# Two edits in a hybrid backbone kernel: GLA's zero-padded queries copied by ScalarE from one product for both directions, and rotary embedding over two token tiles an instruction

## The chip, the core and the metric

The kernel runs on one core of one Trainium2 chip. The time is in device microseconds, from one execution of the whole program; a stated time is the median of several runs. The engines are TensorE (PE, with its weight loads shown apart as PEld), VectorE (DVE), ScalarE (ACT), GpSimd (POOL) and SyncE (SP, which issues the transfers). Each engine works through its own instructions strictly in the order in which the program holds them.

## The reference

Two layers of a diffusion backbone, over 1024 latent tokens and 256 context tokens of width 1024. Each layer norms and modulates its input, projects it with one matrix of 2,592 columns, and feeds three groups of heads: a convolution module (width 31), windowed attention with rotary embedding (8 query heads of 64, 2 key heads), and gated linear attention (GLA) in both directions. Their outputs go through gates and one output projection. The parts that the change touches are these:

```
def _apply_rope(x, cos, sin):
    half = ATTN_HEAD_DIM // 2                       # 32
    rot = concatenate([-x[..., half:], x[..., :half]], axis=-1)
    return x * cos + rot * sin

def _gla_chunked(q, k, v, log_a, s0):               # chunks of 64 tokens, 4 heads, dk = 32, dv = 64
    b = cumsum(log_a within the chunk)
    q_in = q * exp(b)
    k_in = k * exp(-b)
    att = where(causal, q_in @ k_in.T, 0)           # per head
    o = att @ v + q_in @ s                          # s: the state that enters the chunk
```

The backward direction does the same on flipped tokens, and the two outputs are added, normed and gated. All of it is in 32-bit floats.

## The kernel before, in words

Tokens come in ten tiles of 128: tiles 0 and 1 are the context, 2 to 9 the latent stream. A projection works on groups of 256 columns (`GROUPS`), whose products are three matmul passes over high and low halves of the operands. Some groups leave their output with columns on the partitions and tokens along the free axis (`t_group`), others with tokens on the partitions, two tiles at a time (`tok_group`). `mix` is a large buffer with columns on the partitions; in it row group 2 holds GLA's queries, 3 its keys, 4 and 5 the running sums b of the forward and the backward direction, 6 and 7 the states and later GLA's output.

The order of all instructions is made by a planner while the program is built. The work is split into lanes (Python generators). `Model` keeps a clock for each engine, with a price for each instruction by its shape, and the time at which each piece of a buffer is written and last touched; `loop` takes, at each step, the ready lane of the lowest priority number, lets it issue up to its next `yield`, and moves on. A lane that yields with no condition goes on when the model thinks that what it issued is done. The prices are fixed formulas: `150 + 2.1 n` ns for a POOL product of n elements a partition, `75 + n / 0.96` for a DVE product, `n / 1.2 + 93` for an ACT instruction that reads SBUF. They know nothing of one engine holding up another at a memory port. If a price changes, the order of all that comes after may change on each engine. The hardware then runs the instructions in that order, with semaphores between engines where one needs another's data.

What lies beside the change in `phase_a`, in both layers: while PE runs the groups 10 (v and the low-rank gate), 8 (GLA's q and k), 5 (attention's k and v), 3 and 4 (attention's q), DVE works through the 62 instructions of the convolution (`conv_taps`, each issued when the model has DVE idle), and lanes of GLA run on all engines.

Rotary embedding: `ev_qk_b` takes a pair of tiles from PSUM to an SM buffer with one ACT copy, turns each latent tile with `rope` on POOL (four instructions a tile: the swapped halves times the sines into a borrowed WR buffer, the tile times the cosines in place, a subtract on the first halves and an add on the second), and sends the pair to DRAM through SP. For group 5 the turned part is 2 heads a tile (K, 128 elements a partition), for groups 3 and 4 it is 4 heads (Q, 256 elements). Context tiles are not turned. There are 4 latent pairs in each of three groups in each of two layers, 24 in all.

GLA: `gla_states` makes the chunk states (it has a POOL product of keys and decay, 128x512, that PE then transposes). `gla_out` makes the output of one token tile; two lanes of it run beside each other, over 10 tiles in layer 0 and 8 in layer 1. For each tile it makes exp(b/16) and exp(-b/16) for both directions in `w` (`ws`, an SM buffer), multiplies the keys into the second two, and multiplies the queries into `qx`, a buffer for each direction in which head h has its 32 partitions filled and the rest stays zero, so that one matmul serves four heads. Then PE makes the scores, DVE masks and adds them, PE makes the output, and further steps norm it.

Nearly every line of the profile says L43: all instructions go through one wrapper, `issue` at line 43. Instructions are told apart by engine, tile names and shapes. Rope is POOL `WR<-SM,SM` (sines), `SM<-SM,SM` (cosines) and `SM<-SM,WR` (subtract, add), with 128x128, 128x128 and 128x64 for K and 128x256, 128x256 and 128x128 for Q. The states' product is POOL `SM<-SM,mix 128x512`; GLA's key products are POOL `SM<-SM,mix 128x128`, its query products DVE `SM<-SM,mix 32x128`, its exponentials ACT `SM<-mix 128x128`. The conv taps are DVE `mix<-U,small,mix 128x1295` in layer 0 and `128x1024` in layer 1.

Of the kernel before, what the change touches and what calls it, by code (L numbers as in the profile page):

```python
# [12 lines left out]
ACTF = mybir.ActivationFunctionType  # L13
ALU = mybir.AluOpType
# [12 lines left out]
def col(t):  # L27
    return t if t < 256 else t + GAP
# [136 lines left out]
class Hybrid:  # L165
# [717 lines left out]
                self.flag(f"v{l}.{i}")  # L883
        return ev

    def rope(self, x, nh, blk, tmp):

        nc = self.nc
        x4 = x.rearrange("p (h a b) -> p h a b", a=2, b=32)
        t4 = tmp.rearrange("p (h a b) -> p h a b", a=2, b=32)  # L890
        cos, sin = [self.rt[:, s * 256 + blk * 32:s * 256 + blk * 32 + 32][:, None, None, :].to_broadcast([128, nh, 2, 32]) for s in range(2)]
        e = nc.gpsimd
        e.tensor_tensor(t4, x4[:, :, ::-1, :], sin, op=ALU.mult)
        e.tensor_tensor(x4, x4, cos, op=ALU.mult)
        e.tensor_tensor(x4[:, :, 0], x4[:, :, 0], t4[:, :, 0], op=ALU.subtract)
        e.tensor_tensor(x4[:, :, 1], x4[:, :, 1], t4[:, :, 1], op=ALU.add)

    def ev_qk_b(self, l, name, dst, nh):

        def ev(i0, p):  # L900
            nc = self.nc
            yield self.need("SM"), self.need("WR", 1, 1), f"rope{l}"
            s, tmp = self.sm(512), self.get("WR")
            s3 = s.rearrange("p (s c) -> p s c", s=2)
            nc.scalar.activation(s3, p, ACTF.Copy)
            yield
            if i0 >= 2:
                for r in range(2):
                    self.rope(s3[:, r, 0:nh * 64], nh, i0 + r - 2, tmp[:, r * 256:r * 256 + nh * 64])
            self.free(tmp)  # L910
            yield
            nc.sync.dma_start(dst[i0:i0 + 2].rearrange("s p c -> p s c"), s3)
            self.free(s)
            for i in (i0, i0 + 1):
                self.flag(f"{name}{l}.{i}")
        return ev
# [204 lines left out]
    def gla_out(self, l, i, qx, v):  # L1121
        nc = self.nc
        o = col(i * 128)
        yield self.need("SM", 2), self.rest(v), f"T{l}.0.{self.hslot(i)[0]}"
        self.load_vz(i, v)
        ws, A = self.sm(512), self.sm(512)
        w = ws.rearrange("p (a t) -> p a t", a=4)
        for d in range(2):
            b = self.mix(4 + d, slice(o, o + 128))
            nc.scalar.activation(w[:, d], b, ACTF.Exp, scale=1.0 / 16.0)  # L1130
            nc.scalar.activation(w[:, 2 + d], b, ACTF.Exp, scale=-1.0 / 16.0)
        yield self.at(ws)
        for d in range(2):
            nc.gpsimd.tensor_tensor(w[:, 2 + d], w[:, 2 + d], self.mix(3, slice(o, o + 128)), op=ALU.mult)
            for h in range(4):
                r = slice(32 * h, 32 * h + 32)
                nc.vector.tensor_tensor(qx[d][r, h], w[r, d], self.mix(2, slice(o, o + 128), r), op=ALU.mult)
        yield None, self.bank_need("tr")
        at = self.bank_get("tr")
        for d in range(2):  # L1140
            for c in range(2):
                nc.tensor.matmul(at[64 * c:64 * c + 64, d * 256:(d + 1) * 256], w[:, 2 + d, 64 * c:64 * c + 64],
                                 qx[d][:, :, 64 * c:64 * c + 64], start=True, stop=True, tile_position=(0, 64 * c))
        yield
        for d in range(2):
            nc.vector.copy_predicated(self.zz[:, d].rearrange("p (h t) -> p h t", h=4),
                                      self.gmask[:, d:d + 1].to_broadcast([128, 4, 64]),
                                      at[:, d * 256:(d + 1) * 256].rearrange("p (h t) -> p h t", h=4))
        self.free(at)
        nc.vector.tensor_tensor(A[:, 0:256], self.zz[:, 0], self.zz[:, 1], op=ALU.add)  # L1150
        yield None, self.bank_need("ac"), self.at(v)
        ob = self.bank_get("ac")
        om = ob[:, 0:256]
        for c in range(2):
            rs = slice(64 * c, 64 * c + 64)
            ch = 2 * i + c
            for h in range(4):
                oo = om[rs, h * 64:(h + 1) * 64]
                kw = dict(tile_position=(0, 64 * c))
                nc.tensor.matmul(oo, qx[0][:, h, rs], self.S(0, ch), start=True, stop=False, **kw)  # L1160
                nc.tensor.matmul(oo, qx[1][:, h, rs], self.S(1, ch), start=False, stop=False, **kw)
                nc.tensor.matmul(oo, A[:, h * 64:(h + 1) * 64], v[:, h, c], start=False, stop=True, **kw)
        yield
        om3 = om.rearrange("p (h v) -> p h v", h=4)
        sq = A[:, 256:512]
        nc.scalar.activation(sq, om, ACTF.Square)
        yield
        ss = self.ti(4)
        nc.vector.tensor_reduce(ss, sq.rearrange("p (h v) -> p h v", h=4), axis=mybir.AxisListType.X, op=ALU.add)
        r = self.rstd(ss, 1.0 / 64.0, 4)  # L1170
        yield
        nc.vector.tensor_tensor(sq.rearrange("p (h v) -> p h v", h=4), om3, r[:, :, None].to_broadcast([128, 4, 64]), op=ALU.mult)
        self.free(ob)
        yield None, self.bank_need("tr")
        tp = self.bank_get("tr")
        for j in range(2):
            nc.tensor.transpose(tp[:, j * 128:(j + 1) * 128], sq[:, j * 128:(j + 1) * 128], self.idf)
        yield
        for j in range(2):
            nc.scalar.activation(self.mix(6 + j, slice(o, o + 128)), tp[:, j * 128:(j + 1) * 128], ACTF.Copy,  # L1180
                                 scale=self.gw[:, l, j:j + 1])
        self.free(tp, ws, A)
        self.flag(f"gla{l}.{i}")
# [573 lines left out]
def _tables():  # L1757
    f = np.float32
    n_freq = 16
    inv = (f(10000.0) ** (-np.arange(n_freq, dtype=f) / f(n_freq))).astype(f)  # L1760
    r = np.repeat(np.arange(16, dtype=f), 64)
    c = np.tile(np.arange(64, dtype=f), 16)
    ang = np.concatenate([r[:, None] * inv, c[:, None] * inv], axis=-1).astype(f)
    rope = np.stack([np.cos(ang), np.sin(ang)]).astype(f)
    rope = rope.reshape(2, 8, 128, 32).transpose(2, 0, 1, 3)
    q = np.arange(128)[:, None]
    k = np.arange(128)[None, :]
    z = np.zeros((128, 128), f)
    prev = np.where(k >= q, 0.0, NEG).astype(f)
    nxt = np.where(k <= q, 0.0, NEG).astype(f)  # L1770
    amask = np.concatenate([z, z, prev, z, nxt], axis=1)
    s = (np.arange(128) % 64)[:, None]
    t = np.arange(64)[None, :]
    gm = np.stack([s <= t, s >= t], axis=1).astype(f).reshape(128, 128)
    sel = np.zeros((128, 2), f)
    for j in range(0, 128, 32):
        sel[j:j + 2] = [[1, 0], [0, 1]]
    return dict(rope=rope, amask=amask, gmask=gm, sel=sel)
# [56 lines left out]
```

## Time and profile before

| | |
|---|---|
| median of 3 runs | 1350.08 us (1346.76 to 1352.33) |
| profiled execution, its time | 1350.69 us |
| its span, from the first to the last instruction | 1348.9 us |
| mean clock granted to TensorE | 0.977 |
| rope and GLA beside the projections, layer 0 | about 185 to 345 us of the span |
| the same, layer 1 | about 894 to 1040 us |

A row of the groups of instructions has: line, engine, operation, output and inputs by tile name, their shapes, the count, then the busy time and the mean ns of one, then the idle time ahead of them and what ended it. A row of a timeline has: start, length, engine, line, operation, tiles and shapes, count, and in brackets the idle time ahead of the first and what ended it. Instructions of one kind in a row are merged, so a length over several of them includes the gaps. A row of waits has: who waited, for whom, total us, how often, the longest. Each number comes from one profiled execution.

### The profile page before, as it was taken

What the parts mean: (1) busy time and instruction counts of PE and PEld (TensorE: products, weight loads), DVE (VectorE), ACT (ScalarE), POOL (GpSimd) and SP (SyncE); (2) the same over time, 40 slices, a digit from 0 to 9 for tenths busy, and PEclk for the clock granted to TensorE, in tenths of its full rate; (3) what the DMA queues carried; (4) which work ended last, traced back from release to release, by engine and by line L of the source; (5) the groups of instructions that cost most, each with busy time, mean ns of one, the idle gap of its engine ahead of it and who ended that gap; (6) DMA issues with size and microseconds to landing.
All of it is one profiled execution on the core that took longest, in us unless ns stands there. A gap on an engine that the chain in (4) does not pass through costs nothing. (4 is left out here: it accounts for less than half of the span.)

```text
span 1348.9 us, 24464 instructions
## 1 busy us (share of the span) xinstructions
PE 1253.7 (93%) x9198; PEld 1089.8 (81%) x9198; DVE 962.9 (71%) x1856; ACT 560.2 (42%) x1251; POOL 542.9 (40%) x769
## 2 busy tenths in 40 slices
PE   5999997889999999899999889988899999999997
PEld 3678886778788777779988879977787888898997
DVE  5835894888556577777776676896966478887864
ACT  3711431112223456456652461341112256676751
POOL 1410065956223334434341132056792335645430
PEclk9999988999999999899999989989999999999999
DMA  9453113222114333432113441113232113311112
GB/s 328 143 151 102 47 32 99 59 73 74 29 32 126 120 102 106 137 106 67 48 40 110 139 168 56 53 40 104 69 81 54 39 43 102 98 44 52 63 36 79
DMA packets 113239, 116.48 MB, mean 86 GB/s; under 512 B 38464, under 2 KB 81760, under 8 KB 113120
## 3 DMA queue, kind: packets, MB, share of 16 engines
q1 hardware_dynamic: 113120, 114.92, 28.2%
q8 instruction: 72, 1.18, 0.4%
q14 instruction: 47, 0.39, 0.1%
HBM read 95.47 MB, written 19.42 MB: 85 GB/s over the span
## 5 line engine op out<-in xcount | busy, mean ns | idle before, releaser
L43 PE MATMUL ps<-H,WS 128*128 128x512 f32 x1344 | 339.1, 399 | 3.6 <-ACT U L43 1.7
L43 PEld LDWEIGHTS ps<-H,WS 128*128 128x128 f32 x1344 | 245.1, 189 | 64.2 <-issue 10.0
L43 PE MATMUL ps<-WS,H 128*128 128x256 f32 x1704 | 258.3, 294 | 8.1 <-DVE H L43 4.7
L43 ACT ACTIVATE SM<-ps 128x512 f32<-128x512 f32 (+3 forms) x180 | 92.6, 517 | 397.8 <-PE ps L43 284.2
L43 PEld LDWEIGHTS ps<-WS,H 128*128 128x128 f32 x1704 | 232.1, 198 | 21.4 <-issue 10.2
L43 PE MATMUL ps<-idr,SM 128*128 128x128 f32 (+1 forms) x1076 | 150.5, 273 | 38.1 <-POOL SM L43 25.5
L43 DVE SCALAR_TENSOR_TENSOR mix<-U,small,mix 128x1295 f32<-128x1295 f32 (+1 forms) x120 | 177.6, 1526 | 0.2
L43 PEld LDWEIGHTS ps<-idr,SM 128*128 128x128 f32 (+1 forms) x1076 | 124.1, 143 | 62.2 <-POOL SM L43 29.6
L43 DVE SCALAR_TENSOR_TENSOR H<-ps,H 128x512 fp32r<-128x512 f32 x160 | 105.7, 681 | 46.3 <-ACT H L43 46.1
L43 ACT ACTIVATE SM<-SM,stat 128x641 f32<-128x641 f32 (+2 forms) x144 | 110.5, 769 | 56.4 <-DVE stat L43 43.0
L43 ACT ACTIVATE H<-ps 128x512 fp32r<-128x512 f32 x176 | 99.4, 597 | 80.5 <-PE ps L43 73.9
L43 POOL TENSOR_TENSOR SM<-SM,SM 128x256 f32<-128x256 f32 (+4 forms) x91 | 72.8, 808 | 149.0 <-ACT SM L43 112.5
L43 POOL TENSOR_TENSOR tir<-tir,mhalf 128x1 f32<-128x1 f32 (+2 forms) x55 | 44.9, 820 | 197.8 <-DVE tir L43 173.4
L43 DVE CUSTOM_DVE_ANT_0 SM<-ps,SM,small 128x640 f32<-128x640 f32 (+2 forms) x128 | 102.3, 809 | 25.5 <-PE ps L43 24.7
L43 POOL TENSOR_TENSOR SM<-SM,WR 128x128 f32<-128x128 f32 (+2 forms) x117 | 90.8, 793 | 21.4 <-DVE SM L43 14.2
L43 PE MATMUL ps<-H,H 128*128 128x256 f32 x552 | 97.5, 286 | 0.0
L43 PE MATMUL ps<-H 128*128 128x512 f32 x320 | 97.0, 409 | 0.2 <-DVE H L43 0.2
L43 PE MATMUL ps<-SM,SM 128*32 128x128 f32 (+4 forms) x764 | 81.3, 295 | 12.5 <-DVE SM L43 7.8
L43 PEld LDWEIGHTS ps<-H,H 128*128 128x128 f32 x552 | 81.6, 189 | 1.4 <-issue 0.4
L43 POOL TENSOR_SCALAR SM<-SM,tir 128x640 f32<-128x640 f32 (+2 forms) x77 | 67.7, 892 | 28.5 <-DVE tir L43 18.0
L43 PE MATMUL ps<-WS,SM 128*128 128x256 f32 x248 | 70.2, 283 | 0.0
L43 PE MATMUL ps<-H,SM 128*128 128x256 f32 x248 | 69.4, 280 | 0.0
(150 smaller groups left out, 2121.9 us busy)
## 6 DMA issues: line engine op xcount, KB each, us to landing
WR<-in_w_in_dram SPq DMA_DIRECT2D x80, 256.0 KB, 3.9
WR<-in_w_mod_dram SPq DMA_DIRECT2D x64, 256.0 KB, 3.1
WR<-in_w_out_dram SPq DMA_DIRECT2D x32, 256.0 KB, 3.4
SM<-vd SPq DMA_DIRECT2D x116, 64.0 KB, 2.4
x<-SM SPq DMA_DIRECT2D x20, 256.0 KB, 2.3
SM<-x SPq DMA_DIRECT2D x20, 256.0 KB, 4.3
qd<-SM SPq DMA_DIRECT2D x18, 256.0 KB, 2.2
mix<-in_x_dram SPq DMA_DIRECT2D x8, 512.0 KB, 8.3
```

The lines of the kernel that those rows point to most:

```text
L43: r = getattr(self._e, op)(*a, **k)
```

## The change

In `rope`, a call now takes both tiles of a pair: the tables' columns of two neighbouring blocks are read as one pattern with a tile axis. There are two products with the sines (one for each half, in place of one with the halves swapped by a negative step), one with the cosines over both tiles, one subtract and one add: five POOL instructions for a pair in place of eight. In `gla_out`, the exponentials take both directions in one ACT instruction; one DVE product multiplies the queries into both directions and another the keys, 128 partitions by 256 elements each; then ACT copies the eight 32-partition pieces into `qx`. POOL has no product in `gla_out` any more.

```diff
-    def rope(self, x, nh, blk, tmp):
-        nc = self.nc
-        x4 = x.rearrange("p (h a b) -> p h a b", a=2, b=32)
-        t4 = tmp.rearrange("p (h a b) -> p h a b", a=2, b=32)
-        cos, sin = [self.rt[:, s * 256 + blk * 32:s * 256 + blk * 32 + 32][:, None, None, :].to_broadcast([128, nh, 2, 32]) for s in range(2)]
-        e = nc.gpsimd
-        e.tensor_tensor(t4, x4[:, :, ::-1, :], sin, op=ALU.mult)
-        e.tensor_tensor(x4, x4, cos, op=ALU.mult)
-        e.tensor_tensor(x4[:, :, 0], x4[:, :, 0], t4[:, :, 0], op=ALU.subtract)
-        e.tensor_tensor(x4[:, :, 1], x4[:, :, 1], t4[:, :, 1], op=ALU.add)
+    def rope(self, x, t, nh, blk):
+        e = self.nc.gpsimd
+        cos, sin = [self.rt[:, s * 256 + blk * 32:s * 256 + blk * 32 + 64].rearrange("p (r b) -> p r b", b=32)[:, :, None, :] for s in range(2)]
+        x5, t5 = [z.rearrange("p s (h a b) -> p s h a b", a=2, b=32) for z in (x, t)]
+        for a in range(2):
+            e.tensor_tensor(t5[:, :, :, a], x5[:, :, :, 1 - a], sin.to_broadcast([128, 2, nh, 32]), op=ALU.mult)
+        x4 = x.rearrange("p s (g b) -> p s g b", b=32)
+        e.tensor_tensor(x4, x4, cos.to_broadcast([128, 2, 2 * nh, 32]), op=ALU.mult)
+        for a, op in ((0, ALU.subtract), (1, ALU.add)):
+            e.tensor_tensor(x5[:, :, :, a], x5[:, :, :, a], t5[:, :, :, a], op=op)
...
-                for r in range(2):
-                    self.rope(s3[:, r, 0:nh * 64], nh, i0 + r - 2, tmp[:, r * 256:r * 256 + nh * 64])
+                self.rope(s3[:, :, 0:nh * 64], tmp.rearrange("p (s c) -> p s c", s=2)[:, :, 0:nh * 64], nh, i0 - 2)
...
-        for d in range(2):
-            b = self.mix(4 + d, slice(o, o + 128))
-            nc.scalar.activation(w[:, d], b, ACTF.Exp, scale=1.0 / 16.0)
-            nc.scalar.activation(w[:, 2 + d], b, ACTF.Exp, scale=-1.0 / 16.0)
-        yield self.at(ws)
-        for d in range(2):
-            nc.gpsimd.tensor_tensor(w[:, 2 + d], w[:, 2 + d], self.mix(3, slice(o, o + 128)), op=ALU.mult)
+        both = self.mix(slice(4, 6), slice(o, o + 128))
+        for a in range(2):
+            nc.scalar.activation(w[:, 2 * a:2 * a + 2], both, ACTF.Exp, scale=(1.0 - 2 * a) / 16.0)
+        yield self.at(ws)
+        for a in range(2):
+            nc.vector.tensor_tensor(w[:, 2 * a:2 * a + 2], w[:, 2 * a:2 * a + 2],
+                                    self.mix(2 + a, slice(o, o + 128))[:, None, :].to_broadcast([128, 2, 128]), op=ALU.mult)
+        yield
+        for d in range(2):
             for h in range(4):
                 r = slice(32 * h, 32 * h + 32)
-                nc.vector.tensor_tensor(qx[d][r, h], w[r, d], self.mix(2, slice(o, o + 128), r), op=ALU.mult)
+                nc.scalar.activation(qx[d][r, h], w[r, d], ACTF.Copy)
```

## The prediction

> **What bounds the kernel now.** The page's first lines come first, and then the list of who waited for whom, for TensorE (PE) alone.
>
> ```profile
> span 1348.9 us, 24464 instructions
> PE 1253.7 (93%) x9198; PEld 1089.8 (81%) x9198; DVE 962.9 (71%) x1856; ACT 560.2 (42%) x1251; POOL 542.9 (40%) x769
> PE ps L43 <- POOL SM L43: 26.4, 14, 8.7
> PE ps L43 <- DVE SM L43: 15.2, 16, 2.0
> ```
>
> PE is busy for 93% of the span, so an edit that takes no matmul away can win at most the 95.2 us in which PE stands (1348.9 - 1253.7), and what a lowered clock costs. The edit touches products on POOL and DVE, and those are the two longest entries of PE's waits: 26.4 and 15.2 us. The timeline of PE shows where they lie; the number in brackets is the idle time ahead of the instruction.
>
> ```profile
> 212.52 1.12 PE L43 MATMUL ps<-idr,SM 128*128 128x128 f32 x4 [8.68 <-POOL SM L43]
> 250.87 0.66 PE L43 MATMUL ps<-idr,SM 128*128 128x128 f32 x4 [4.09 <-POOL SM L43]
> 298.82 0.65 PE L43 MATMUL ps<-SM,SM 128*64 128x256 f32 x4 [1.87 <-DVE SM L43]
> 301.35 1.12 PE L43 MATMUL ps<-SM,SM 128*64 128x256 f32 x4 [1.87 <-DVE SM L43]
> 918.30 0.66 PE L43 MATMUL ps<-idr,SM 128*128 128x128 f32 x4 [2.96 <-POOL SM L43]
> 967.44 1.82 PE L43 MATMUL ps<-SM,SM 128*64 128x256 f32 x12 [0.92 <-POOL SM L43]
> 969.95 0.65 PE L43 MATMUL ps<-SM,SM 128*64 128x256 f32 x4 [0.70 <-DVE SM L43]
> 988.64 0.41 PE L43 MATMUL ps<-idr,SM 128*128 128x128 f32 x2 [1.05 <-DVE SM L43]
> ```
>
> The first four lie in layer 0 and the last four in layer 1, both times in the stretch where rope, the conv taps and GLA run beside the projections. What POOL and DVE did ahead of the first wait:
>
> ```profile
> 197.49 1.27 POOL L43 TENSOR_TENSOR WR<-SM,SM 128x128 f32<-128x128 f32 x1 [4.49 <-ACT SM L43]
> 198.84 1.60 POOL L43 TENSOR_TENSOR SM<-SM,SM 128x128 f32<-128x128 f32 x1
> 200.52 3.02 POOL L43 TENSOR_TENSOR SM<-SM,WR 128x64 f32<-128x64 f32 x2
> 206.97 3.01 POOL L43 TENSOR_TENSOR SM<-SM,WR 128x64 f32<-128x64 f32 x2
> 209.94 3.75 POOL L43 TENSOR_TENSOR SM<-SM,mix 128x512 f32<-128x512 f32 x2
> 213.66 0.45 POOL L43 TENSOR_TENSOR WR<-SM,SM 128x128 f32<-128x128 f32 x1
> 195.40 15.94 DVE L43 SCALAR_TENSOR_TENSOR mix<-U,small,mix 128x1295 f32<-128x1295 f32 x10
> ```
>
> PE waits for gla_states' product at 209.94, and that stands on POOL behind a K pair of rope: eight instructions from 197.49 to 209.98, 1.56 us each. The same 128x128 instruction takes 0.45 us at 213.66, after the taps. While DVE issues ten taps in 15.94 us (1.59 each), POOL gets one instruction through per tap, whatever its size between 64 and 128 elements. So in this stretch the **number** of POOL instructions sets the time, more than their elements do.
>
> **Part one, rope.** A pair of tiles goes from eight instructions to five: two sine products and a subtract and an add over both tiles, and one cosine product twice as long. Elements stay the same. Without taps beside it, a Q pair's instruction and one of 512 elements are these:
>
> ```profile
> 260.51 0.73 POOL L43 TENSOR_TENSOR WR<-SM,SM 128x256 f32<-128x256 f32 x1
> 231.32 1.29 POOL L43 TENSOR_TENSOR WS<-WR,WS 128x512 fp32r<-128x512 f32 x1 [2.59 <-ACT WS L43]
> ```
>
> 256 to 512 elements costs 0.56 us more, so 2.2 ns an element and 0.17 us fixed. Three instructions fewer are 0.5 us a pair there, 24 pairs in both layers, 12 us of POOL, and hidden: PE does not wait for POOL in such places. Beside taps, three instructions fewer are worth three tap slots. K pair at 197.49: five slots, four of 1.6 and one, now 256 elements, of about 1.9 (below), are 8.3 us in place of 12.5: **4.2 us** off the 8.68. The next late thing is the product itself, 3.75 us for the two directions, so about 4.5 us of the wait stay.
>
> The second wait:
>
> ```profile
> 237.51 0.92 POOL L43 TENSOR_TENSOR WR<-SM,SM 128x256 f32<-128x256 f32 x1
> 241.00 2.00 POOL L43 TENSOR_TENSOR WR<-SM,SM 128x256 f32<-128x256 f32 x1
> 243.08 1.89 POOL L43 TENSOR_TENSOR SM<-SM,SM 128x256 f32<-128x256 f32 x1
> 248.29 2.52 POOL L43 TENSOR_TENSOR SM<-SM,mix 128x512 f32<-128x512 f32 x1
> 240.64 11.54 DVE L43 SCALAR_TENSOR_TENSOR mix<-U,small,mix 128x1295 f32<-128x1295 f32 x6
> 208.00:212.00 4.00, 0.00 (x0) 0.00 (x0) 3.34 (x3) 0.00 (x0) 4.00 (x3) 0.50 0.22 72
> 275.00:300.00 25.00, 21.46 (x224) 19.39 (x220) 21.54 (x37) 5.82 (x18) 14.92 (x20) 0.99 0.20 55
> 375.00:400.00 25.00, 25.00 (x154) 20.86 (x153) 15.70 (x37) 5.74 (x13) 8.01 (x8) 1.00 0.15 44
> 252.00:256.00 4.00, 3.97 (x31) 3.29 (x32) 3.15 (x9) 0.16 (x1) 3.77 (x6) 0.63 0.22 50
> ```
>
> The Q pair fills POOL from 237.51 to 248.29. Two sine products of about 1.0 us, a cosine of 512 elements of some 2.0 (1.29 alone, 2.52 beside a tap at 248.29), and two of 1.95 (the mean of 2.00 and 1.89) make 7.9 us in place of 10.8: **2.8 us** off the 4.09. The last four rows are stretches of the span: length, busy time of PE, its weight loads, DVE, ACT and POOL, then the clock granted to PE, DMA share and GB/s. The clock stood at half in the long wait and at a mean of 0.63 after the second, which cost 0.37 x 4 = 1.5 us of PE. A wait of 1.3 us would not bring this (a wait of 1.87 us lies in the stretch at 0.99), so **1.5 us** more. After the first wait the clock stays lowered, as 4.5 us still exceeds 4.09.
>
> In layer 1 the wait of 2.96 us ends on the same product behind a K pair.
>
> ```profile
> 915.04 1.32 POOL L43 TENSOR_TENSOR SM<-SM,SM 128x128 f32<-128x128 f32 x1
> 916.99 1.26 POOL L43 TENSOR_TENSOR SM<-SM,mix 128x512 f32<-128x512 f32 x1
> ```
>
> Three slots of 1.32 us are 4.0 us, more than the wait: **3.0 us**. Rope's product goes out by the same SP transfer as before, only earlier, and the WR buffer that it borrows is back earlier for the weights.
>
> The Trainium skill ("SBUF — State Buffer", "Who interferes with whom") says that a DVE instruction with two SBUF inputs and a GpSimd instruction that reads SBUF hold each other out for the whole of the instruction. By that a tap and a 128-element product would take turns, and the slot would be 1.59 + 0.45 = 2.04 us, so the K pair would give 1.9 us more than by the row's 1.6; here the row decides, since 1.6 us is what the slots took.
>
> **Part two, GLA.** Of each of the 18 token tiles it takes eight 32x128 products from DVE and two 128x128 from POOL, and puts two 128x256 products on DVE and eight 32x128 copies on ACT; four exponentials of 128 become two of 256.
>
> ```profile
> L43 DVE TENSOR_TENSOR SM<-SM,mix 32x128 f32<-32x128 f32 x144 | 61.9, 430 | 4.6 <-ACT SM L43 2.4
> L43 POOL TENSOR_TENSOR SM<-SM,mix 128x128 f32<-128x128 f32 x36 | 18.0, 522 | 11.8 <-issue 6.3 <-ACT SM L43 5.0 <-POOL SM L43 0.6
> L43 DVE TENSOR_TENSOR SM<-SM 128x256 f32<-128x256 f32 x18 | 8.7, 486 | 0.8
> L43 ACT ACTIVATE SM<-SM 128x256 f32<-128x256 f32 x14 | 5.4, 415 | 5.0 <-DVE SM L43 4.9
> 265.31 1.70 ACT L43 ACTIVATE SM<-mix 128x128 f32<-128x128 f32 x8
> 290.01 4.52 DVE L43 TENSOR_TENSOR SM<-SM,mix 32x128 f32<-32x128 f32 x8
> 296.05 5.15 DVE L43 TENSOR_TENSOR SM<-SM,mix 32x128 f32<-32x128 f32 x8
> 294.57 1.57 DVE L43 SCALAR_TENSOR_TENSOR mix<-U,small,mix 128x1295 f32<-128x1295 f32 x1
> ```
>
> DVE: 144 x 0.430 = 61.9 us go, 36 x 0.486 = 17.5 us come, so 44 us less. POOL loses 18.0 us. ACT: eight 128-element exponentials in a row take 1.70 us, 0.21 each; a copy of 32x128 has as many elements a partition, so eight copies are 1.7 us a tile. The exponentials fall from 0.85 to at most 2 x 0.415 = 0.83. ACT gets 18 x 1.7 = 31 us more, on an engine that is busy 42%. What hides them is that ACT stands idle most of this time (it is busy 5.82 us in the 25 from 275); without that cover it is the 31 us.
>
> On the path lie the two waits of 1.87 us. The eight products of a tile last 4.52 us from 290.01, a tap follows, and those of the next tile last 5.15 us from 296.05; PE waits for both halves of them. After: two products of 0.49 to 1.0 us for either tile, with the 1.57 us tap still between them or behind, put the second tile's at about 294.5 at the latest (290.0 + 2.0 + 1.6 + 1.0), and its copies 1.7 us later at 296.2, ahead of the 296.95 at which PE began to wait (298.82 - 1.87). Both waits would go, 3.7 us; I take **3.0 us**, as the extra hand-over to ACT and back, and what stands ahead on ACT, is not in any row here. In layer 1 the 0.92 us wait for POOL's product goes with it, and the 0.70 us for DVE's: **1.6 us**. The 1.05 us at 988.64 I leave in.
>
> The copies wait on DVE at the head of ACT's queue. Queued behind them are the PSUM evacuations of the Q groups, GLA's squares and the scaled copies to mix; for the evacuations PE's next bank waits.
>
> **The sum** is 4.2 + 2.8 + 1.5 + 3.0 + 3.0 + 1.6 = 16.1 us. Every edit also changes the planner's costs, so it lays out all instructions behind the first K pair anew: its prices for a tile are 683 in place of 1,667 ns on DVE, nothing in place of 838 on POOL, and some 2,210 in place of 800 on ACT. How the new order meets the other waits no row shows; bounds are the PE idle outside the eight waits, 95.2 - 22.1 = 73 us, with either sign, and I take 3 us of loss, because work that is earlier on PE meets weights and v tiles that come when they come. So 13 us faster than the profiled execution's 1350.7: 1337.7; the median of the runs lies 0.6 us under that execution, which gives **1337 us**.
>
> **The rivals.**
> *The gain is given back* (0.25). POOL stops being last, and PE waits for the next thing in the same places: GLA states' own products (3.75 us at 209.94), a v tile, an evacuation. For it: PE's waits are many and short, 14 for POOL and 16 for DVE. Against: behind the stretch PE runs full (25.00 of 25 us from 375), so time won is kept. If only the layer 1 wait and half of the rest are left, 3.0 + 0.5 x 4.2 = 5 us are won and 3 to 5 lost: 1350.1 - 1 = 1349. That the longer instructions cost what the short ones did (a cosine of 512 elements holding DVE as long) ends here too.
> *Slower: ACT becomes the hand-over that PE waits for* (0.12). Place: every gla_out tile, where copies wait for DVE's products, which wait for a tap of 1.57 us. It decides from where ACT's queue stands at its head longer than PE's spare bank lasts; then each of 18 tiles costs its 1.7 us, 31 us, against 11.5 us won by rope: 1350.1 + 19 = 1369, or 1357 if 11 tiles do. Against it: the 5.82 us of 25 would rise to about 11.
> *More than forecast* (0.08). POOL's lag goes as a whole: 8.68 + 4.09 + 2.96 of waits, 1.5 us of clock behind each of the first two, and the other waits on GLA's products (3.7 + 1.6 us) are 24 us; with 2 us from a better order, 1324.
>
> **How the numbers follow.** The forecast holds 0.55, with 1328 to 1343 as its own range (9 us more won, or 6 more lost, by the new order). 0.5%, 6.8 us, is about what a measurement of this kernel can tell from no change. Faster by more: 0.55 + 0.08 = 0.63; within: 0.25; slower by more: 0.12. For eight in ten, 1324 to 1354.
>
> **What would show it.** Rope: POOL's tensor products fall by 72 + 36 in number, and its busy time by 40 to 50 us; PE's wait for POOL falls from 26.4 to under 15 us. If the K pair's five instructions still take 12 us beside taps, the slot reading is wrong. GLA: DVE about 44 us less busy, ACT about 31 more; if PE's list of waits shows ACT's SM tiles with over 10 us more than now, the slower rival holds. If POOL and DVE waits fall and the time does not, the re-laid order took it.

## The result, and the profile after

The kernel after took a median of **1326.88 us** (1324.96 to 1329.01, 4 runs); the kernel before, with one more run of it, 1348.42 us (1345.08 to 1352.33). The ratio is **0.984**, with a 95% interval of 0.9807 to 0.9873: 21.5 us faster. Forecast were 13 us; the time lies in the range on record, just below the forecast's own 1328 to 1343.

The first lines of the page of after:

```profile
span 1323.2 us, 24344 instructions
PE 1245.2 (94%) x9198; PEld 1085.2 (82%) x9198; DVE 931.4 (70%) x1756; ACT 600.4 (45%) x1355; POOL 490.8 (37%) x657
```

The span fell by 25.7 us in these two executions. PE issues the same 9198 matmuls, yet its busy time fell by 8.5 us (1253.7 to 1245.2); the other 17.2 us are idle time (95.2 to 78.0). So a third of the gain is not shorter waits but the same work done in less time, and the clock granted to PE rose with it, from a mean of 0.977 to 0.985. PE's list of waits (who waited, for whom, total us, times, longest):

```profile
PE ps L43 <- POOL SM L43: 14.2, 9, 3.8
...
PE ps L43 <- ACT SM L43: 11.4, 14, 4.6
...
PE ps L43 <- DVE SM L43: 6.3, 6, 2.1
```

POOL's entry fell from 26.4 to 14.2 us and that of DVE's SM tiles from 15.2 to 6.3; ACT's rose from 8.1.

The timeline of PE shows what stays of the waits that the prediction named:

```profile
206.11 1.11 PE L43 MATMUL ps<-idr,SM 128*128 128x128 f32 x4 [3.76 <-POOL SM L43]
...
275.95 0.65 PE L43 MATMUL ps<-SM,SM 128*64 128x256 f32 x4 [0.17 <-ACT SM L43]
277.24 0.65 PE L43 MATMUL ps<-SM,SM 128*64 128x256 f32 x4 [0.64 <-ACT SM L43]
...
422.62 0.96 PE L43 MATMUL ps<-H,WS 128*128 128x512 f32 x3 [0.49 <-DVE mix L43]
...
873.62 0.44 PE L43 MATMUL ps<-idr,SM 128*128 128x128 f32 x2 [3.19 <-POOL SM L43]
...
895.18 1.12 PE L43 MATMUL ps<-idr,SM 128*128 128x128 f32 x4 [2.44 <-POOL SM L43]
```

The wait of 8.68 us is 3.76 now; the one of 4.09 is gone, with no wait for POOL between 207 and 305; GLA's two of 1.87 us are 0.17 and 0.64, and they end on ACT's copies. In layer 1 the wait of 2.96 is still 2.44. The row at 873.62 is a wait on a product of the states that the change does not touch, and the one at 422.62 lies in layer 0 behind the stretch of rope and GLA. In before the same matmuls, and one behind layer 1's stretch, are these:

```profile
439.67 1.19 PE L43 MATMUL ps<-H,WS 128*128 128x512 f32 x4 [0.49 <-DVE mix L43]
...
896.37 0.44 PE L43 MATMUL ps<-idr,SM 128*128 128x128 f32 x2 [3.17 <-POOL SM L43]
...
1101.72 0.96 PE L43 MATMUL ps<-H,WS 128*128 128x512 f32 x3 [0.54 <-DVE stat L43]
```

The same matmul in two executions is a landmark: the difference of its starts is what has been won up to there. Layer 0's stretch has won 17.1 us (439.67 to 422.62). Where layer 1's stretch begins, it is 22.8 of the 25.7 us (896.37 to 873.62), so 5.7 us came in between, where the edit touches nothing. From there on no more than some 3 us came.

The timelines of POOL and, in the last row, of DVE, of after, ahead of the first wait:

```profile
195.99 2.25 POOL L43 TENSOR_TENSOR WR<-SM,SM 128x128 f32<-128x128 f32 x2 [1.78 <-ACT SM L43]
198.32 1.89 POOL L43 TENSOR_TENSOR SM<-SM,SM 128x256 f32<-128x256 f32 x1
200.29 3.28 POOL L43 TENSOR_TENSOR SM<-SM,WR 128x128 f32<-128x128 f32 x2
203.54 2.52 POOL L43 TENSOR_TENSOR SM<-SM,mix 128x512 f32<-128x512 f32 x1
194.68 10.26 DVE L43 SCALAR_TENSOR_TENSOR mix<-U,small,mix 128x1295 f32<-128x1295 f32 x6
```

The K pair's five instructions take 7.6 us (195.99 to 203.57) where eight took 12.5. Six taps stand beside them, 1.71 us each. The product of 512 elements is what is late next, as predicted.

### The profile page after: what moved, and what is told of

Its sections match the earlier page's. It is cut to its first block, busy times and chain, and to the rows that moved or that the text cites. A ratio compares the mean times of both kernels' runs of the same rounds, so it can differ in the third digit from the quotient of the medians.

```text
span 1323.2 us, 24344 instructions
## 1 busy us (share of the span) xinstructions
PE 1245.2 (94%) x9198; PEld 1085.2 (82%) x9198; DVE 931.4 (70%) x1756; ACT 600.4 (45%) x1355; POOL 490.8 (37%) x657
## 5 line engine op out<-in xcount | busy, mean ns | idle before, releaser
L43 PEld LDWEIGHTS ps<-WS,H 128*128 128x128 f32 x1704 | 229.4, 195 | 20.0 <-issue 10.3
L43 PE MATMUL ps<-idr,SM 128*128 128x128 f32 (+1 forms) x1076 | 150.1, 272 | 26.8 <-POOL SM L43 14.2
L43 PEld LDWEIGHTS ps<-idr,SM 128*128 128x128 f32 (+1 forms) x1076 | 124.3, 143 | 51.3 <-POOL SM L43 17.2
L43 POOL TENSOR_TENSOR SM<-SM,SM 128x128 fp32r<-128x128 f32 (+3 forms) x58 | 58.6, 1018 | 130.8 <-ACT SM L43 108.9
L43 ACT ACTIVATE SM<-SM 32x128 f32<-32x128 f32 (+4 forms) x200 | 72.0, 368 | 41.2 <-DVE SM L43 33.5
L43 POOL TENSOR_SCALAR SM<-SM,tir 128x640 f32<-128x640 f32 (+2 forms) x77 | 64.7, 853 | 34.5 <-DVE tir L43 23.9
L43 POOL TENSOR_TENSOR SM<-SM,WR 128x256 f32<-128x256 f32 (+2 forms) x66 | 69.0, 1051 | 16.0 <-DVE SM L43 5.8
L43 POOL TENSOR_TENSOR WR<-SM,SM 128x256 f32<-128x256 f32 (+1 forms) x48 | 45.5, 969 | 72.1 <-ACT SM L43 72.1
```

The source lines that it names most:

```text
L43: r = getattr(self._e, op)(*a, **k)
```

## The experiments

Two things are mixed in the change: the instructions (the work), and the order that the planner makes of all instructions once their prices differ. The planner sees each instruction through its model, so the two can be parted: the model is shown one version, and the engines are given the other. In the diffs `seen` is the model alone and `run` the engine alone. All ratios are to the kernel before, run beside it on the same chip.

### The new work in the old order, and the old work in the new one

```diff
             if i0 >= 2:
+                seen, run = Shadow(nc).gpsimd, nc.nc.gpsimd
...
+                    self.rope_old(seen, s3[:, r, 0:nh * 64], nh, i0 + r - 2, tmp[:, r * 256:r * 256 + nh * 64])
+                self.rope_new(run, s3[:, :, 0:nh * 64], t3, nh, i0 - 2)
```

The same is done with GLA's exponentials, products and copies. The second kernel swaps `seen` and `run`, and keeps the new `yield` behind the products.

> All new instructions (rope over two tiles, GLA with two products and eight copies), but the planner is shown the old ones, so that PE, SP and all else stand in the order of the kernel before. Theory 1, the work itself: POOL gets through a K pair in five tap slots in place of eight, and GLA's products come sooner; the sum without the new order, 16 us, so 1332 us, with PE's wait for POOL under 15 us. Rival, the new order did it: within 5 us of the kernel before, 1343 to 1350. Rival, ACT as the hand-over: 1355 or more, with PE's wait for ACT's SM tiles over 18 us.

> All old instructions, but the planner is shown the new ones, so that PE, SP and all else stand in the order of the changed kernel. Theory 1: the order by itself wins nothing or costs 3 us, 1348 to 1352. Rival, the new order did it: most of the 21 us are here, 1327 to 1333. Between: the measured 21.5 us less the 16 of the sum are the order's, 1343.

Measured: the new work in the old order 1332.71 us, ratio 0.9877 (0.9843 to 0.991), 16.2 us faster. The old work in the new order 1358.91 us, ratio 1.007 (1.0044 to 1.0097), 10 us slower, which is more than any of the three expectations had. The first lines of the page of the new work in the old order:

```profile
span 1329.8 us, 24315 instructions
PE 1246.1 (94%) x9198; PEld 1081.2 (81%) x9198; DVE 935.3 (70%) x1748; ACT 601.8 (45%) x1359; POOL 511.2 (38%) x661
```

Its timeline of PE:

```profile
206.32 1.11 PE L43 MATMUL ps<-idr,SM 128*128 128x128 f32 x4 [3.80 <-POOL SM L43]
...
240.93 0.66 PE L43 MATMUL ps<-idr,SM 128*128 128x128 f32 x4 [0.21 <-POOL SM L43]
...
286.06 0.65 PE L43 MATMUL ps<-SM,SM 128*64 128x256 f32 x4 [0.64 <-ACT SM L1175]
...
321.98 0.65 PE L43 MATMUL ps<-SM,SM 128*64 128x256 f32 x4 [1.66 <-ACT SM L1175]
...
427.77 0.96 PE L43 MATMUL ps<-H,WS 128*128 128x512 f32 x3 [0.49 <-DVE mix L43]
...
877.37 0.69 PE L43 MATMUL ps<-idr,SM 128*128 128x128 f32 x2 [3.17 <-POOL SM L43]
...
898.62 0.66 PE L43 MATMUL ps<-idr,SM 128*128 128x128 f32 x4 [2.45 <-POOL SM L43]
...
1079.72 0.96 PE L43 MATMUL ps<-H,WS 128*128 128x512 f32 x3 [0.55 <-DVE stat L43]
```

Since PE's order is the same in both, the gain can be read off at every matmul:

| up to | gain |
|---|---|
| the first wait (212.52 to 206.32) | 6.2 us |
| the second wait (250.87 to 240.93) | 9.9 us |
| the second of GLA's waits of 1.87 us (301.35 to 286.06) | 15.3 us |
| behind layer 0's stretch (439.67 to 427.77) | 11.9 us |
| where layer 1's stretch begins (896.37 to 877.37) | 19.0 us |
| behind layer 1's stretch (1101.72 to 1079.72) | 22.0 us |
| the end of the span | 19.1 us |

Three things stand in this table. In layer 0's stretch the gain rises to 17.4 us (306.24 to 288.83), and then 5.3 are lost again: PE waits for ACT's copies (L1175 in this kernel) at GLA's later tiles, 1.66 us at 321.98 and 0.4 to 0.6 at each of four groups of matmuls behind it, and from 324 to 328 its granted clock stands at 0.57. In before the longest wait at the same matmuls is 0.55 us. Over the whole span PE waits 7.1 us, nine times, for these copies, which is most of the 8.4 us that it waits less for DVE's SM tiles (15.2 to 6.8). Between the two stretches 7.1 us are won although neither rope nor GLA's output runs there; about 5 of them are matmuls that run in less time. And behind layer 1's stretch 2.9 us are lost, again outside the change: PE waits 1.99 us at 1205.32 for ACT, which waits for the keys' transfer from DRAM 3.29 us, where in before it waits 1.16.

The new order with the old work puts the eight small products of two tiles behind one another. Its timelines of PE and, in the second and third row, of DVE and POOL:

```profile
260.26 1.65 PE L43 MATMUL ps<-SM,SM 128*64 128x256 f32 x8 [2.71 <-POOL SM L1168]
253.79 8.56 DVE L1171 TENSOR_TENSOR SM<-SM,mix 32x128 f32<-32x128 f32 x16
259.71 1.89 POOL L1168 TENSOR_TENSOR SM<-SM,mix 128x128 f32<-128x128 f32 x4
```

That order was laid out for products that the planner prices at 683 ns a tile, and for no key products on POOL. Here 16 products hold DVE for 8.56 us, and PE waits for the first of POOL's key products, which begin at 259.71, behind two pairs of rope. So by these runs an order is good or bad for a given work, and has no price of its own.

### Rope alone and GLA alone

Rope's five instructions alone, once at the price of the old eight, so that the order stays, and once at their own price:

```diff
+        self.nc.price = (1500 + 2.1 * 384 * nh) / 5.0
...
+        self.nc.price = None
```

> The new rope alone, at the price of the old one, so that every engine has the order of the kernel before and POOL's rope alone differs. Theory 1: the first, second and fifth waits shrink by 4.2, 2.8 and 3.0 us and 1.5 us of clock comes back, 11.5 us, 1337 us; PE's wait at about 212 falls from 8.7 to about 4.5 us. Rival, the waits move on to the next thing: 1343 or more.

> The new rope alone, at its own price, so with an order of its own. Theory 1: 11.5 us less, give or take 3 for the order, 1334 to 1340. If the order matters more than the work it differs from the run with the old order by over 5 us.

Measured: 1341.24 us in the old order, ratio 0.9941 (0.9919 to 0.9962), 7.7 us faster where 11.5 were expected; 1362.79 us in its own, ratio 1.0096 (1.0058 to 1.0133). The same instructions are 21.5 us apart by order alone. In the old order the second wait is gone (0.14 us left) and the first, at 206.77, is 5.05 us. Part of this is lost again at GLA's products on DVE: the first wait of 1.87 us, at 298.82 in before, is 3.52 us there, at 291.78.

In rope's own order PE's waits for POOL stay low, at 16.8 us, and those for DVE's SM tiles rise from 15.2 to 27.2. One of them, from the timelines of PE and, in the second row, of DVE:

```profile
992.90 0.48 PE L43 MATMUL ps<-SM,SM 128*64 128x64 f32 x2 [3.94 <-DVE SM L43]
986.19 5.51 DVE L43 SCALAR_TENSOR_TENSOR mix<-U,small,mix 128x1024 f32<-128x1024 f32 x3
```

PE waits 3.94 us for DVE's masks and adds behind three taps. The planner's lower price for rope moved DVE's queue. That this queue suits GLA's old form badly is a reading of this row and the list; no run shows how much of the 21.5 us it is.

GLA alone, in the old order (edit: the model is shown the old exponentials and products, the engines get the new ones and the copies) and in its own:

```diff
+            seen.gpsimd.tensor_tensor(w[:, 2 + d], w[:, 2 + d], self.mix(3, slice(o, o + 128)), op=ALU.mult)
...
+                run.scalar.activation(qx[d][r, h], w[r, d], ACTF.Copy)
```

> The new GLA products and copies alone, rope as before, everything in the order of the kernel before. If the two parts add up, this is what was left between the rope run and the full one in the same order, 1341.2 - 1332.7 = 8.5 us: 1340 us. By the prediction's sum 3.0 + 1.6 us: 1344. Rival, GLA is worth something only once rope has cleared POOL: under 3 us, 1346 or more. PE's wait for DVE's SM tiles falls from 15.2 to under 10 us if the hand-over to ACT works.

> The new GLA alone, at its own price and so in its own order. In the old order it won 0.2%. If an order of its own is as costly as rope's was (21 us), 1355 to 1365; if the DVE price that now fits is what makes the new order good, 1335 to 1343.

Measured: 1345.47 us, ratio 0.998 (0.9958 to 1.0001), and 1352.88 us, ratio 1.004 (0.9996 to 1.0084): next to nothing, either way. In the old order PE's waits for DVE's SM tiles fall to 9.8 us, and those for POOL stay at 25.1. PE's timeline there:

```profile
252.85 1.11 PE L43 MATMUL ps<-idr,SM 128*128 128x128 f32 x4 [4.51 <-POOL SM L43]
...
298.62 0.65 PE L43 MATMUL ps<-SM,SM 128*64 128x256 f32 x4 [0.33 <-ACT SM L1163]
...
336.89 0.65 PE L43 MATMUL ps<-SM,SM 128*64 128x256 f32 x4 [1.66 <-ACT SM L1163]
```

GLA's two waits of 1.87 us go (0.33 left), and those behind rope stay whole, 8.49 and 4.51 us. But at the tiles behind them PE now waits for ACT's copies, 1.66 us at 336.89, and 4.9 us in eight such waits over the span. That takes back most of the 5.4 us that PE waits less for DVE, and by this list it is why the part is worth so little alone.

The two parts alone add up to 0.59% + 0.20%, about 10.5 us, and both together in the same order won 16.2 us. The intervals are wide (5.1 to 10.9, 0 to 5.7 and 12.1 to 21.2 us). In the profiled executions PE's idle time nearly adds up, 6.6 and 3.6 us less alone and 11.5 together; the surplus is in its busy time, 1.9 and 2.0 us less alone and 7.6 together. That the parts need each other is thus not shown.

### Are the taps the cause? Before and the new work, both without them

The slot reading says that POOL's instructions are slow because of the taps. If so, a change that saves POOL instructions is worth nothing once the taps are gone. All but two of the convolution's 62 instructions in each layer are left out; the model still sees them, so the order is that of before:

```diff
-                    nc.vector.scalar_tensor_tensor(acc, src, self.p_conv_w(l, j, s), acc, op0=ALU.mult, op1=ALU.add)
+                    nc.issue("dve", "scalar_tensor_tensor", (acc, src, self.p_conv_w(l, j, s), acc), {})
```

> The kernel before, in the same order, but of the 62 convolution instructions of a layer only the first two run, so the convolution is left out. Theory, POOL waits for a gap between taps: rope's 128x256 products fall from a mean of 1.0 to under 0.8 us, the K pair takes under 4 us in place of 12.5, PE's wait for POOL falls from 26.4 to under 12 us, and the time falls by 12 to 25 us. Rival, POOL's own fixed cost: rope's products keep their mean of 1.0 us and PE's wait for POOL stays over 20 us.

> All new instructions in the order of the kernel before, again with only the first two of a layer's 62 convolution instructions, so the convolution is left out. Theory, the taps make the gain: without them the new work wins under 6 us over the old work, in place of 16. Rival, fewer instructions are worth the same anywhere: 12 us or more.

Measured: before without taps 1302.86 us, ratio 0.9659 (0.9624 to 0.9693); the new work in the old order without taps 1304.93 us, ratio 0.9673 (0.963 to 0.9717). Without taps the new work wins nothing that can be measured, with them 16.2 us. The K pair of before without taps, first and last row of eight instructions in POOL's timeline:

```profile
194.91 0.46 POOL L43 TENSOR_TENSOR WR<-SM,SM 128x128 f32<-128x128 f32 x1 [4.34 <-ACT SM L43]
...
197.64 0.61 POOL L43 TENSOR_TENSOR SM<-SM,WR 128x64 f32<-128x64 f32 x2
```

Eight instructions take 3.3 us (194.91 to 198.25), not 12.5, and PE's waits for POOL's SM tiles are 3.3 us in all, not 26.4. The taps cost the kernel 43.6 us (1346.41 us for before beside these runs, less 1302.86) although DVE is busy for 71% of the span only. That holds both what they take from POOL and what they take in DVE's own queue.

### Can the slots be used further?

If the number of POOL instructions is what counts, three a pair should be better than five. ACT writes the swapped halves from PSUM, the first negated, and POOL is left with two products and one add:

```diff
+                for a in range(2):
+                    nc.scalar.activation(t5[:, :, :, a], p5[:, :, :, 1 - a], ACTF.Copy, scale=2.0 * a - 1.0)
...
+        e.tensor_tensor(t4, t4, sin, op=ALU.mult)
         e.tensor_tensor(x4, x4, cos, op=ALU.mult)
...
+        e.tensor_tensor(x4, x4, t4, op=ALU.add)
```

It was run in its own order, and with the model shown five instructions, so that the order is that of after; after itself was run again beside the second.

> The changed kernel, but ACT writes the swapped halves, the first negated, straight from PSUM into the borrowed buffer, so that rope has three POOL instructions a pair (times sines, times cosines, add) in place of five, and ACT two more. Theory: two slots fewer beside taps; the wait of 3.8 us at about 206 falls under 1.5 us and the one of 2.4 us in layer 1 goes, 4 to 6 us with their clock: 1322 us in the same order; its own order can move that by 10 us either way. Rival, ACT is now too late: PE's wait for ACT's SM tiles rises from 11.4 to over 16 us.

> Rope in three POOL instructions with ACT writing the swapped halves, every engine else in the order of the changed kernel. Theory, two tap slots fewer a pair: PE's waits for POOL fall from 14.2 to about 10 us and the time by 3 to 5 us against the changed kernel, 1322 to 1324. Rival, what POOL still holds up is not rope: within 2 us of the changed kernel.

> The changed kernel once more, for comparison in one batch: 0.984 of the kernel before, 0.981 to 0.987.

Measured: 1329.72 us, ratio 0.9856 (0.9816 to 0.9896), and 1330.05 us, ratio 0.9899 (0.9861 to 0.9938); after again 1328.27 us, ratio 0.9877 (0.9842 to 0.9912). Three instructions are no faster than five. The K pair of three in the order of after, from POOL's timeline:

```profile
195.93 1.98 POOL L905 TENSOR_TENSOR WR<-WR,SM 128x256 f32<-128x256 f32 x1 [2.11 <-ACT WR L932]
197.87 2.00 POOL L906 TENSOR_TENSOR SM<-SM,SM 128x256 f32<-128x256 f32 x1
199.94 1.87 POOL L907 TENSOR_TENSOR SM<-SM,WR 128x256 f32<-128x256 f32 x1
```

Its list of PE's waits:

```profile
PE ps L43 <- ACT SM L43: 15.3, 20, 5.3
...
PE ps L43 <- POOL SM L43: 11.5, 9, 3.2
```

The pair takes 5.9 us in place of 7.6, three slots of 1.96 us. PE's waits for POOL's SM tiles fall by 2.7 us against after, and those for ACT's rise by 3.9 (3.1 and 2.9 against after again). So what POOL no longer holds up ACT does, most of it at GLA's copies, up to 1.53 us there where after has 0.64; the expected 3 to 5 us did not come.

The last run held each tap back until the model had POOL idle too, with the work of after:

```diff
-                yield self.idle("dve", 300)
+                yield self.idle("dve", 300), self.idle("pool", 0)
```

> The changed kernel, but a conv tap is issued only where the planner has POOL idle too, not DVE alone; the same instructions in another order. Theory, taps and POOL products hold each other up: PE's wait for POOL falls from 14.2 to under 10 us and up to half of the 43 us that the taps cost comes back, 1310 to 1322 us. Rival, the planner prices POOL too low to keep them apart, or the convolution comes late for the gates: 1325 to 1340, with PE waits for DVE's U and SM tiles.

Measured: 1342.85 us, ratio 0.9978 (0.9952 to 1.0004), slower than after. Its waits for POOL, 12.5 us, are little below after's 14.2, and PE waits 4.5 us once for DVE's U tiles, which the rival had named. The rule changes the order of everything, and the rope pairs above show what that can cost; it was not tried with the rest of the order held.

## Why the prediction was right, and where it was wrong

**The mechanism held.** The number of POOL instructions beside taps sets the time: five of the K pair took 7.6 us (8.3 forecast), eight without taps 3.3. The predicted signs came: POOL's instructions fell by 112, of which rope and GLA explain the forecast 108; its busy time fell by 52 us (forecast 40 to 50); PE's wait for POOL fell to 14.2 (forecast under 15). With the old order held, the last two are weaker: 31.7 us of busy time, and a wait of 16.5. The first wait's 4.2 us came as 4.9, with 3.76 left (4.5 forecast); the second wait's 2.8 (10.8 less 7.9 is 2.9) came as 4.09, the whole of it; GLA's 3.0 in layer 0 as 2.9 (3.74 less 0.81).

**The slower rival fell.** PE's wait for ACT's SM tiles went from 8.1 to 11.4, not over 10 us more. The groups' rows of after show that the prices on ACT and DVE were nonetheless too low:

```profile
L43 DVE TENSOR_TENSOR SM<-SM,mix 128x256 f32<-128x256 f32 x36 | 26.0, 772 | 8.6 <-ACT SM L43 8.6
L43 ACT ACTIVATE SM<-SM 32x128 f32<-32x128 f32 x144 | 44.3, 307 | 12.1 <-DVE SM L43 10.2
```

A new product took 772 ns, not 486, and a copy 307 ns, not 212; DVE lost 31.5 us of busy time and not 44, ACT gained 40 us and not 31. In after both lay in cover, save for waits of 0.2 to 0.6 us on ACT at some GLA tiles. With the old order held the cover was thinner: 7.1 us of waits for the copies.

**The sum of 16.1 us was near the mark in each stretch, and in part by luck.** The new work in the old order measures just this sum, 16.2 us in its runs, 19.1 in its profile. By the landmarks, layer 0's stretch brought 11.9 us, where the terms are 4.2 + 2.8 + 1.5 + 3.0 = 11.5, and layer 1's 3.0 (19.0 to 22.0), where they are 3.0 + 1.6 = 4.6. The remaining 7.1 us won and 2.9 lost lie outside both, and no term stands for them. On the way from 439.67 to 896.37 of before the other two kernels in the same order differ too: rope alone loses 1.1 us there, GLA alone wins 5.4. So this is no fixed worth of either part, and what causes it is open.

**Failed: the copies, put at nothing beyond the first tiles.** The prediction worked out the hand-over to ACT in layer 0 at the two waits of 1.87 us alone, and there it held. With the old order the gain reached 17.4 us, 5.9 more than the terms, and PE's waits for the copies of the later tiles, with the clock behind them, then took 5.3 back. That the two errors nearly cancel is luck.

**Failed: the 3.0 us of layer 1.** "Three slots of 1.32 us are 4.0 us, more than the wait": 2.45 of 2.96 us stayed, and 2.44 in after. POOL's timeline of after there:

```profile
886.33 2.11 POOL L43 TENSOR_TENSOR WR<-SM,SM 128x128 f32<-128x128 f32 x2 [2.88 <-ACT SM L43]
...
890.20 2.72 POOL L43 TENSOR_TENSOR SM<-SM,WR 128x128 f32<-128x128 f32 x2
892.88 2.25 POOL L43 TENSOR_TENSOR SM<-SM,mix 128x512 f32<-128x512 f32 x1
```

The pair takes 6.6 us (886.33 to 892.92), where in before it took 8.1:

```profile
908.93 0.70 POOL L43 TENSOR_TENSOR WR<-SM,SM 128x128 f32<-128x128 f32 x1 [2.71 <-ACT SM L43]
...
916.43 0.59 POOL L43 TENSOR_TENSOR SM<-SM,WR 128x64 f32<-128x64 f32 x2
```

So 1.5 us were saved, not 4.0: in before the first instruction had taken 0.70 us and the last two 0.59 together, no full slots. Of this the product of 512 elements takes 1.0 back: in before it ran behind the last of the taps in 1.26 us, and now, earlier, it meets one and takes 2.25.

**Failed: that a wait of 1.87 us costs no clock.** The 1.5 us behind the second wait came (the gain goes from 9.9 us at the wait to 11.4 at 259 of before). But "a wait of 1.87 us lies in the stretch at 0.99" was read from too wide a stretch. In stretches of 4 us, the kernel before behind its two waits of 1.87 us, with 0.65 us of matmuls between them (columns: length, busy time and count of PE, weight loads, DVE, ACT and POOL, granted clock, DMA share, GB/s):

```profile
296.00:300.00 4.00, 1.60 (x12) 0.97 (x11) 3.92 (x7) 0.00 (x0) 3.76 (x6) 0.92 0.01 2
300.00:304.00 4.00, 2.65 (x11) 1.93 (x12) 3.91 (x8) 0.00 (x0) 0.97 (x3) 0.50 0.34 98
304.00:308.00 4.00, 4.00 (x50) 3.78 (x49) 3.96 (x5) 0.00 (x0) 0.00 (x0) 0.73 0.00 1
```

That is 1.60 x 0.08 + 2.65 x 0.50 + 4.00 x 0.27 = 2.5 us of PE's work lost, which no term held; with GLA's waits gone, it is gone (by the landmarks 2.1 us, from 15.3 to 17.4). In the profiled executions PE's busy time fell by 7.6 us with the old order and by 8.5 with the new. With the old order about 5 us of this lie between the two stretches, where the edit touches nothing, and no run isolates their cause.

The Trainium skill ("TensorE: Matmul & The Clock Gate", "Part 1: The HAM clock gate") says that the clock is halved after an idle window of about 3.4 us, and that this window is free-running and does not start anew with the kernel. The half clock behind the wait of 4.09 us agrees with that. The two waits of 1.87 us with 0.65 us of matmuls between them are shorter than such a window, and the clock fell to 0.50 all the same. A single wait of 2.44 us, shorter still, was followed by a lowered clock in one execution and an equal one by none in another. These two stretches are of after and then of the new work in the old order, behind a wait of 2.44 and one of 2.45 us:

```profile
896.00:900.00 4.00, 4.00 (x37) 3.67 (x36) 0.82 (x4) 0.70 (x2) 2.56 (x5) 0.73 0.49 117
```

```profile
896.00:900.00 4.00, 1.55 (x14) 1.39 (x13) 1.44 (x2) 1.29 (x3) 3.23 (x4) 1.00 0.40 114
900.00:904.00 4.00, 4.00 (x48) 3.34 (x48) 0.76 (x3) 0.01 (x1) 1.82 (x4) 1.00 0.37 83
```

A wait of the same length cost clock in one and none in the other, and in before the wait of 2.96 us cost none (1.00 from 918 to 922). A window that runs freely would do this. So a fixed length between 1.87 and 4.09 us, by which the prediction gave or withheld the clock's cost, is not borne out.

**Failed: the 3 us of loss for the new order.** With the new work the order of after gives 0.984 and 0.9877 in two sets of runs, the old order 0.9877: no loss that can be seen. In the profiled executions the new order is ahead by 5.1 us behind layer 0's stretch (427.77 to 422.62), where it waits for GLA's copies 1.4 us in all and the old order 4.6; after again agrees with after within 0.7 us over that stretch. With the old work the same order costs 10 us, and rope alone in its own order loses 21.5 us against the old one: within the bound of 73 us, but an effect of order and work together, not a fixed sum. The forecast of 13 us is thus the 16.2 us of the work less these 3; what lies between 16.2 and the 21.5 measured is either the order, for which the 5.1 us speak, or the scatter between sets of runs, as after gained 16.7 us (1345.01 to 1328.27) in the second.

**The rivals.** "The gain is given back" did not come, though it describes rope alone in its own order and GLA alone. "More than forecast", at 1324 us, came nearest in time, but not in its reason: 3.76 and 2.44 us of POOL's lag are still there. Open remains whether after's order is better than the old one for the new work beyond the scatter, and what changes PE's busy time between the two stretches.

## What to carry to other kernels

Where two engines hold each other up, count instructions on the one that has the short ones, and check by leaving out the other engine's work: it shows at once what the contention costs and whether a change is aimed at it. Where a planner orders the program, measure a change in the old order too, since order alone moved one and the same work by 21.5 us, and a part may be a loss alone and a gain with its partner. Price a wait with the clock behind it, read in stretches of a few microseconds.

## What the runs showed of the hardware that was not expected

- A POOL instruction of up to 256 elements beside taps costs about one tap: 1.56 us at 64 and 128 elements in before (taps of 1.59), 1.96 at 256 with three instructions a pair (taps of 1.90). The states' product of 512 elements takes 2.52. Without taps these are 0.30, 0.46, 0.73 and 1.29.
- In the old order, longer POOL instructions slow the taps in return. These rows of the groups are of before and of the new work in the old order:

```profile
L43 DVE SCALAR_TENSOR_TENSOR mix<-U,small,mix 128x1295 f32<-128x1295 f32 x60 | 97.6, 1669 | 0.1
```

```profile
L43 DVE SCALAR_TENSOR_TENSOR mix<-U,small,mix 128x1295 f32<-128x1295 f32 x60 | 105.4, 1800 | 0.0
```

  The taps of layer 0 took 131 ns more each, 7.8 us in all. Most of it is rope's: with rope alone in that order a tap takes 1761 ns, with GLA alone 1684. In the order of after they did not slow down (1659 ns). So fewer and longer instructions on POOL are not always free for DVE.
